# Output projections of a hybrid attention block in a score tile, and the differential tiles' results transposed within the next tile

## The chip, the cores and the metric

One core of a Trainium2 chip runs the whole kernel. The metric is the device time of one execution in microseconds (us). The kernel before takes 808.14 us, the median of three runs (807.63 to 808.69).

## The reference

One decoder block over x of 1024 tokens by 1024 features, in float32. A normalised stream is projected, the columns are split into two groups of heads, each group's result is gated, and one output projection adds both to x:

```python
h = rms_norm(x, norm_g[layer])
proj = h @ w_in[layer]
dq, dk, dv, dz, nq, nkv, nz, ng = jnp.split(proj, IN_SPLITS, axis=-1)
...
o_diff = diff_attention(dq, dk, dv, lam, diff_slopes)
o_diff = rms_norm(o_diff, diff_subln_g[layer]) * (1.0 - lam_init)
o_diff = o_diff.transpose(0, 2, 1, 3).reshape(B, T, DIFF_WIDTH) * jax.nn.silu(dz)
...
o_nsa = g[0] * o_cmp + g[1] * o_slc + g[2] * o_win
o_nsa = o_nsa.transpose(0, 3, 1, 2, 4).reshape(B, T, NSA_WIDTH) * jax.nn.silu(nz)
x = x + jnp.concatenate([o_diff, o_nsa], axis=-1) @ w_out[layer]
```

Differential attention has four heads of two causal softmax maps each; its result is softmax(first) - lambda softmax(second), times a value of width 128, and every head's result is divided by its root mean square. The native sparse attention (NSA) has eight query heads and three branches: compressed blocks, selected blocks, and a window of 512.

## The kernel before

The core works in three phases. Until about 440 us it projects the stream. Then a loop over eight tiles of 128 query tokens does NSA. At last a loop over the same eight tiles, from tile 7 down to tile 0 (`order`), does differential attention; tile `qt` sees `qt + 1` blocks of 128 keys, so tile 7 is the widest.

Both attention loops use `softmax_pair`: for two maps, TensorE computes scores into score tiles (L465, tiles S), as two matmuls for each piece since a query is kept as a high and a low part, QH and QL. VectorE adds the position bias and takes the extremum (L469, `nm`; a small second instruction reads the accumulated value), and ACT takes the exponential (L471). In the differential loop the two maps of a head are combined: VectorE works out the factor (L774, L775), POOL (L778, L779) and VectorE (L781) combine one half each. Then TensorE transposes the probabilities (L786), ACT or VectorE evicts them (L522, L520), and TensorE multiplies them by the values into a value tile O (L790). In NSA the transposes are L649 and the value matmuls L654.

When O of a differential tile is done, a norm chain runs: ACT squares it (L795), VectorE sums (L797) and mixes (L799, L800), POOL takes a power (L802), VectorE scales the factor and multiplies (L803, L804), and POOL multiplies by the gate (L806). `finish` then transposes the result on TensorE (L155), splits it in a high part `ch` (ACT, L748) and a low part `cl` (VectorE, L749), and calls `out_proj`: for each of two halves of 512 columns 12 matmuls (L502 to L504), an add to `xt` on VectorE (L505), which came by DMA, and a store (L506). `finish` of a tile is called after the heads of the next tile. In the NSA loop `out_proj` of a tile is called after the next tile's value matmuls.

PSUM has eight banks: two score tiles of two banks each (`S_tile`), two tiles for transposes of one bank each (`T_tile`), and two value tiles of one bank each (`A_tile`). O is a value tile, and so is each half of a projection, and the four transposes of the NSA gates (L696).

`load_w_out` loads the output weights in four row blocks and splits each of eight units in a high part on ACT (L488) and the rest on POOL or VectorE (L490). The order of the instructions on each engine is set by a scheduler, which places them by the program's order, its own estimates and the buffers; so the order written in the code is a priority and not the order on the engines.

Of the kernel before, what the change touches and what calls it, by code (L numbers as in the profile page):

```python
# [10 lines left out]
AF = mybir.ActivationFunctionType  # L11
# [16 lines left out]
def block_kernel(ctx: ExitStack, tc: tile.TileContext, x, norm_g, w_in, dq_g, dk_g, lq1, lk1, lq2, lk2,  # L28
                 sub_g, nq_g, nk_g, cmp_pos, cmp_w1, cmp_b1, cmp_w2, w_out, out):
    nc = tc.nc  # L30
    x = x[0]
    out = out[0]
# [13 lines left out]
    def S_tile():  # L46
        return psS.tile([128, 1024], F32, tag="S", name="S")
# [4 lines left out]
    def A_tile():  # L52
        return psA.tile([128, 512], F32, tag="A", name="A")

# [42 lines left out]
    xa_d = dram.tile([NT, 128, 1024], F32, name="xa_d")  # L97
# [69 lines left out]
    with ExitStack() as p1:  # L167
        big = p1.enter_context(tc.tile_pool(name="p1big", bufs=1))
# [4 lines left out]
        st = ctxS.enter_context(tc.tile_pool(name="p1s", bufs=2))  # L173
# [32 lines left out]
        def mm_tokens(hi, lo, tt, n):  # L206
            A = acc_tile()
            t0 = 128 * tt
            for k in range(8):
                a, b = xh[:, k, t0:t0 + 128], xl[:, k, t0:t0 + 128]  # L210
                nc.tensor.matmul(A[:, :n], a, hi[:, k, :n], start=(k == 0), stop=False)  # L211
                nc.tensor.matmul(A[:, :n], a, lo[:, k, :n], start=False, stop=False)  # L212
                nc.tensor.matmul(A[:, :n], b, hi[:, k, :n], start=False, stop=(k == 7))  # L213
            return A

# [32 lines left out]
        with ExitStack() as pc:  # L248
# [5 lines left out]
            for tt in range(NT):  # L254
# [7 lines left out]
                A = mm_tokens(*w_c0, tt, 384)  # L262
# [42 lines left out]
        for tt in range(NT):  # L305
            A = mm_tokens(*w_c1, tt, 408)
# [81 lines left out]
        for th in range(2):  # L388
            for g in range(4):
                A = acc_tile()  # L390
                for k in range(8):
                    a, b = hi[:, k, 128 * g:128 * g + 128], lo[:, k, 128 * g:128 * g + 128]
# [17 lines left out]
        for tt in range(NT):  # L410
            A = mm_tokens(*w_dz, tt, 512)
# [40 lines left out]
        def softmax_pair(QH, QL, heads, slopes, Ks, w0, biases, n, ssums, Ps):  # L452

            if n <= 512:
                S = S_tile()
                S = S[:, :512], S[:, 512:]
            else:
                S = S_tile(), S_tile()

            o = 128 if n == 640 else 0  # L460
            parts = [(c, min(c // 512 * 512 + 512, o + max(n, 256))) for c in range(o, o + n, 512 - o)][:2]
            for a in range(2):
                for c0, c1 in parts:
                    for Q in (QH, QL):
                        nc.tensor.matmul(S[a][:, c0:c1], Q[:, heads[a]], Ks[a][:, w0 + c0 - o:w0 + c1 - o],  # L465
                                         start=Q is QH, stop=Q is QL)
            for a in range(2):
                nm = small.tile([128, 1], F32, tag="nm", name="nm", bufs=8)
                nc.vector.tensor_tensor_reduce(out=Ps[a][:, :n], in0=S[a][:, o:o + n], in1=biases[a], scale=-slopes[a],  # L469
                                               scalar=3e38, op0=ALU.add, op1=ALU.min, accum_out=nm)  # L470
                nc.scalar.activation(Ps[a][:, :n], Ps[a][:, :n], AF.Exp, scale=-1.0, bias=nm, accum_out=ssums[a])  # L471

        def load_w_out(pool, raws, k0, tag, bufs):

            woh = pool.tile([128, 4, 1024], F32R, name="woh")
            wol = pool.tile([128, 4, 1024], F32R, name="wol")
            for k in range(4):

                rows = raws.tile([128, 1024], F32, tag=tag, name="wrow", bufs=bufs)
                if k0:  # L480
                    for j in range(2):
                        r0 = 512 + 256 * j + 64 * k
                        nc.sync.dma_start(rows[64 * j:64 * j + 64], w_out[r0:r0 + 64])
                else:
                    pools["wo_last"] = nc.sync.dma_start(rows, w_out[128 * k:128 * k + 128])
                for nh in range(2):
                    c = slice(512 * nh, 512 * nh + 512)
                    nc.scalar.activation(woh[:, k, c], rows[:, c], AF.Copy)  # L488
                    eng = nc.vector if k0 else nc.gpsimd
                    eng.tensor_tensor(wol[:, k, c], rows[:, c], woh[:, k, c].bitcast(F32), op=ALU.subtract)  # L490
            return woh, wol

        def out_proj(pool, ch, cl, wo, src, dst, xbufs):

            woh, wol = wo
            xt = pool.tile([128, 1024], F32, tag="xt", name="xt", bufs=xbufs)
            nc.sync.dma_start(xt, src)
            for nh in range(2):
                A = A_tile()
                c = slice(512 * nh, 512 * nh + 512)  # L500
                for k in range(4):
                    nc.tensor.matmul(A, ch[:, k], woh[:, k, c], start=(k == 0), stop=False)  # L502
                    nc.tensor.matmul(A, ch[:, k], wol[:, k, c], start=False, stop=False)  # L503
                    nc.tensor.matmul(A, cl[:, k], woh[:, k, c], start=False, stop=(k == 3))  # L504
                nc.vector.tensor_tensor(xt[:, c], A, xt[:, c], op=ALU.add)  # L505
                nc.sync.dma_start(dst[:, c], xt[:, c])  # L506
# [156 lines left out]
        pools, early = {}, {}  # L663
        for tt in range(NT):
# [5 lines left out]
            A = mm_tokens(*w_dv, tt, 512)  # L670
# [10 lines left out]
    with ExitStack() as p2:  # L681
        pools["w"] = p2.enter_context(tc.tile_pool(name="p2w", bufs=1))
        pools["rings"] = 2
        keep = p2.enter_context(tc.tile_pool(name="p2k", bufs=1))
        pools["ring"] = p2.enter_context(tc.tile_pool(name="p2r", bufs=1))
        st = p2.enter_context(tc.tile_pool(name="p2s", bufs=2))
        vsw = pools["ring"].tile([128, 2, NT, 128], F32, name="vsw")
        nc.sync.dma_start(vsw, v_d)
        wo_n = load_w_out(keep, pools["w"], 4, "bs", 2)
        pending = None  # L690
        for qt in range(NT):
            t0 = 128 * qt
            QH, QL, nzt, gate, pg, rep = nxt
            Tp = A_tile()
            for g in range(4):
                nc.tensor.transpose(Tp[:, 128 * g:128 * g + 128], pg[:, g].rearrange("p k c -> p (k c)"), ident)  # L696
            pT = pT_tile("pcT")
            nc.scalar.activation(pT, Tp, AF.Copy)
            O = A_tile()
            nc.tensor.matmul(O, vcbd, pT, start=True, stop=False)  # L700
            if qt + 1 < NT:
                nxt = cmp_branch(qt + 1)


            for br in (1, 0):
                for gp in range(2):
                    Ps = early.pop((qt, br, gp), None) or nsa_softmax(qt, br, gp, QH, QL, gate, rep)
                    nsa_values(qt, br, gp, Ps, O)
            if pending:
                out_proj(*pending)  # L710
            nc.vector.tensor_tensor(nzt, O.rearrange("p (g q) -> p g q", g=4), nzt, op=ALU.mult)
            ch = st.tile([128, 4, 128], F32R, tag="ch", name="ch")
            cl = st.tile([128, 4, 128], F32R, tag="cl", name="cl")
            nc.scalar.activation(ch, nzt, AF.Copy)
            nc.gpsimd.tensor_tensor(cl, nzt, ch.bitcast(F32), op=ALU.subtract)
            pending = (st, ch, cl, wo_n, x[t0:t0 + 128], xa_d[qt], 1)
        O_first = A_tile()
        out_proj(*pending)

    nctx.close()  # L720


    with ExitStack() as p3:
        kp = p3.enter_context(tc.tile_pool(name="p3k", bufs=1))
        p2p = p3.enter_context(tc.tile_pool(name="p3p", bufs=1))
        pools["rings"] = 1
        big = p3.enter_context(tc.tile_pool(name="p3big", bufs=1))
        st = p3.enter_context(tc.tile_pool(name="p3s", bufs=1))
# [4 lines left out]
            nc.sync.dma_start(dv[:, tt], dv_d[tt])  # L733
        for m in range(4):
            k_load(dkB[:, m], "dk", 4 + m)
        wo_d = load_w_out(big, p2p, 0, "P2", 7)

        def loads(qt):
            Q = q_stack(qs_d["dq"][qt])
# [4 lines left out]
        def finish(sq, qt):  # L744
            T3 = transposed(sq, 4)
            ch = st.tile([128, 4, 128], F32R, tag="ch", name="ch", bufs=2)
            cl = st.tile([128, 4, 128], F32R, tag="cl", name="cl", bufs=2)
            nc.scalar.activation(ch, T3, AF.Copy)  # L748
            nc.vector.tensor_tensor(cl, T3, ch.bitcast(F32), op=ALU.subtract)  # L749
            out_proj(st, ch, cl, wo_d, xa_d[qt], out[128 * qt:128 * qt + 128], 2)  # L750

        post = None
        order = (7, 6, 5, 4, 3, 2, 1, 0)
        nxt = loads(order[0])
        for i, qt in enumerate(order):
            t0 = 128 * qt
            n = t0 + 128
# [8 lines left out]
            for h in range(4):  # L766
# [6 lines left out]
                c = small.tile([128, 1], F32, tag="dc", name="dc")  # L773
# [8 lines left out]
                for k4 in range(0, qt + 1, 4):  # L782
# [5 lines left out]
                    for k in range(kn):  # L788
                        kt = k4 + k
                        nc.tensor.matmul(O[:, 128 * h:128 * h + 128], pT[:, 128 * k:128 * k + 128],  # L790
                                         dv[:, kt, 128 * h:128 * h + 128], start=(kt == 0), stop=(kt == qt))
            if post:
                finish(*post)
            sq = st.tile([128, 512], F32, tag="sq", name="sq", bufs=2)
            nc.scalar.activation(sq, O, AF.Square)  # L795
            ss = small.tile([128, 4], F32, tag="oss", name="oss")
# [8 lines left out]
                                    r[:, :, None].to_broadcast([128, 4, 128]), op=ALU.mult)  # L805
            nc.gpsimd.tensor_tensor(sq, sq, gz, op=ALU.mult)  # L806
            post = (sq, qt)
        finish(*post)


_INS = ['x', 'norm_g', 'w_in', 'diff_q_norm_g', 'diff_k_norm_g', 'diff_lambda_q1', 'diff_lambda_k1',
# [20 lines left out]
```

## Time and profile before

| | |
|---|---|
| median of three runs | 808.14 us |
| the profiled execution, device time | 807.29 us |
| its span | 805.6 us |
| TensorE matmuls busy | 770.8 us (96%) |
| VectorE busy | 516.6 us (64%) |
| ACT busy | 356.6 us (44%) |
| POOL busy | 329.1 us (41%) |

PE is TensorE's matmuls, PEld its weight loads, which lie beside them; DVE is VectorE, SP issues DMAs. An instruction's duration is from its start to its modelled end. Matmuls are pipelined, so that the distance between two starts is shorter than the duration.

### The profile page before, as it was taken

How to read it: one execution, taken by the hardware profiler on the slowest of the kernel's cores; microseconds unless marked ns; L12 is line 12 of the kernel's file. 1: busy time of each engine (PE TensorE's matmuls, PEld its weight loads, DVE VectorE, ACT ScalarE, POOL GpSimd, SP SyncE). 2: the span in 40 equal slices, each digit the busy share in tenths (PEclk: the TensorE clock that was granted, in tenths of full speed). 3: DMA queues.
4: the chain of work that ended last, by engine and by line, in shares of the span. 5: the costliest groups of instructions: out<-in, count | busy, mean ns of one | idle time of the engine just before them, and what ended most of it. 6: DMA issues, size and time to landing. Idle time of an engine off the chain costs nothing. (4 is left out here: it accounts for less than half of the span.)

```text
span 805.6 us, 13024 instructions
## 1 busy us (share of the span) xinstructions
PE 770.8 (96%) x4457; PEld 640.9 (80%) x4457; DVE 516.6 (64%) x1239; ACT 356.6 (44%) x803; POOL 329.1 (41%) x393
## 2 busy tenths in 40 slices
PE   5999999999999999999979999999999999999997
PEld 4899988888888888888757778777777668998885
DVE  4643864488634548941487687786866287789843
ACT  6443322241323223101487557565647276766410
POOL 5816272250625526020256443443342227755321
PEclk9999999999999999999999999999999999999999
DMA  8538675472433545177494232341321815556233
GB/s 286 170 58 244 165 228 140 107 195 100 138 102 112 153 100 136 40 184 207 139 216 123 84 106 81 106 91 56 80 65 34 248 34 183 159 141 172 74 130 111
DMA packets 89297, 106.68 MB, mean 132 GB/s; under 512 B 15120, under 2 KB 62352, under 8 KB 89104
## 3 DMA queue, kind: packets, MB, share of 16 engines
q1 hardware_dynamic: 89232, 105.86, 47.4%
q8 instruction: 35, 0.57, 0.3%
q14 instruction: 30, 0.25, 0.1%
HBM read 72.27 MB, written 33.55 MB: 131 GB/s over the span
## 5 line engine op out<-in xcount | busy, mean ns | idle before, releaser
L471 ACT ACTIVATE P<-P,nm 128x128 f32<-128x128 f32 (+7 forms) x136 | 101.4, 748 | 42.6 <-DVE nm L469 39.0
L203 POOL TENSOR_TENSOR wlo<-raw,whi 128x512 fp32r<-128x512 f32 (+2 forms) x64 | 85.7, 1363 | 53.1 <-ACT whi L202 51.3
L522 ACT ACTIVATE pT<-Tp 128x512 f32<-128x512 f32 (+3 forms) x118 | 66.3, 573 | 72.9 <-PE Tp L649 60.4
L138 POOL TENSOR_TENSOR r<-ss,neghalf 128x8 f32<-128x8 f32 (+2 forms) x41 | 51.0, 1244 | 112.6 <-DVE ss L136 107.6
L211 PE MATMUL S<-whi,xh 128*128 128x512 f32 (+2 forms) x224 | 86.5, 386 | 0.6 <-ACT xh L244 0.6
L211 PE MATMUL A<-whi,xh 128*128 128x512 f32 (+2 forms) x224 | 86.8, 388 | 0.0
L213 PE MATMUL A<-whi,xl 128*128 128x512 f32 (+2 forms) x224 | 86.4, 386 | 0.0
L212 PE MATMUL S<-wlo,xh 128*128 128x512 f32 (+2 forms) x224 | 86.3, 385 | 0.0
L213 PE MATMUL S<-whi,xl 128*128 128x512 f32 (+2 forms) x224 | 86.0, 384 | 0.0
L212 PE MATMUL A<-wlo,xh 128*128 128x512 f32 (+2 forms) x224 | 85.6, 383 | 0.0
L618 POOL TENSOR_SCALAR P<-P,ssum 128x128 f32<-128x128 f32 (+7 forms) x72 | 52.2, 743 | 76.4 <-DVE ssum L614 44.2
L469 DVE CUSTOM_DVE_ANT_0 P<-S,D 128x128 f32<-128x128 f32 (+7 forms) x96 | 60.3, 661 | 22.7 <-PE S L465 14.1
L465 PE MATMUL S<-nsaK,QH 128*128 128x384 f32 (+2 forms) x192 | 68.2, 363 | 0.7 <-DVE nm L469 0.7
L654 PE MATMUL A<-pT,vsw 128*64 128x256 f32 x528 | 65.4, 386 | 2.0 <-ACT P L471 1.2
L465 PE MATMUL S<-nsaK,QL 128*128 128x384 f32 (+2 forms) x192 | 60.4, 329 | 0.0
L618 POOL TENSOR_SCALAR Pw<-Pw,ssum 128x640 f32<-128x640 f32 (+3 forms) x56 | 39.8, 730 | 47.7 <-DVE ssum L614 39.8
L163 DVE RECIPROCAL e<-e 128x512 f32<-128x512 f32 (+1 forms) x18 | 57.1, 3175 | 0.5
L520 DVE COPY pT<-Tp 128x512 f32<-128x512 f32 (+3 forms) x62 | 38.5, 620 | 28.3 <-PE Tp L649 28.2
L202 ACT ACTIVATE whi<-raw 128x512 fp32r<-128x512 f32 (+2 forms) x64 | 36.5, 606 | 44.1 <-DMA raw<-in_w_in_dram 38.1
L654 PEld LDWEIGHTS A<-pT,vsw 128*64 128x64 f32 x528 | 34.6, 136 | 25.3 <-ACT pT L522 2.7
L502 PE MATMUL A<-woh,ch 128*128 128x512 f32 x128 | 51.7, 404 | 1.9 <-ACT ch L748 1.5
L504 PE MATMUL A<-woh,cl 128*128 128x512 f32 x128 | 50.3, 395 | 0.1
(189 smaller groups left out, 1772.4 us busy)
## 6 DMA issues: line engine op xcount, KB each, us to landing
raw<-in_w_in_dram SPq DMA_DIRECT2D x48, 256.0 KB, 3.1
xt<-in_x_dram SPq DMA_DIRECT2D x16, 512.0 KB, 3.8
w<-in_cmp_w_dram SPq DMA_DIRECT2D x16, 256.0 KB, 3.8
QH<-nqs_d SPq DMA_DIRECT2D x16, 256.0 KB, 5.3
QL<-nqs_d SPq DMA_DIRECT2D x16, 256.0 KB, 6.6
xa_d<-xt SPq DMA_DIRECT2D x16, 256.0 KB, 2.0
QH<-dqs_d SPq DMA_DIRECT2D x16, 256.0 KB, 5.3
QL<-dqs_d SPq DMA_DIRECT2D x16, 256.0 KB, 7.1
```

The source lines that it names most:

```text
L163: nc.vector.reciprocal(e, e)
L203: nc.gpsimd.tensor_tensor(l_, r_, h_.bitcast(F32), op=ALU.subtract)
L211: nc.tensor.matmul(A[:, :n], a, hi[:, k, :n], start=(k == 0), stop=False)
L212: nc.tensor.matmul(A[:, :n], a, lo[:, k, :n], start=False, stop=False)
L213: nc.tensor.matmul(A[:, :n], b, hi[:, k, :n], start=False, stop=(k == 7))
L465: nc.tensor.matmul(S[a][:, c0:c1], Q[:, heads[a]], Ks[a][:, w0 + c0 - o:w0 + c1 - o], start=Q is QH, stop=Q is QL)
L469: nc.vector.tensor_tensor_reduce(out=Ps[a][:, :n], in0=S[a][:, o:o + n], in1=biases[a], scale=-slopes[a], scalar=3e38, op0=ALU.add, op1=AL ...
L471: nc.scalar.activation(Ps[a][:, :n], Ps[a][:, :n], AF.Exp, scale=-1.0, bias=nm, accum_out=ssums[a])
L502: nc.tensor.matmul(A, ch[:, k], woh[:, k, c], start=(k == 0), stop=False)
L522: nc.scalar.activation(pT[:, :n], Tp[:, :n], AF.Copy)
L618: nc.gpsimd.tensor_scalar(P[:, :n], P[:, :n], ssum[:, g2, j:j + 1], 1.0, op0=ALU.mult, op1=ALU.mult)
L654: nc.tensor.matmul(O[64 * j:64 * j + 64, 256 * gp:256 * gp + 256], vsw[:, br, k0 + kt, 64 * j:64 * j + 64], pT[:, 256 * j:256 * j + 256], ...
```

## The change

`out_proj` takes one score tile and uses its two halves, where it took two value tiles. `finish` no longer calls it: it is called after the second head of the next tile, returns its arguments, and the projection is called at the end of that tile, so a tile's projection is asked for at the end of the next tile but its transposes in the middle of it; the last projections come after the loop. `load_w_out` becomes a generator that yields before each unit. The NSA weights are still split at once, the differential weights one unit per head from tile 6 on, each copy on ACT placed behind the exponential issued last. In the changed file the lines are L508 to L510 for the projection's matmuls, L511 for its add, L655 and L660 for NSA's transposes and values, L797 and L801 for the differential ones.

```diff
-                nc.scalar.activation(Ps[a][:, :n], Ps[a][:, :n], AF.Exp, scale=-1.0, bias=nm, accum_out=ssums[a])
+                exped[0] = nc.scalar.activation(Ps[a][:, :n], Ps[a][:, :n], AF.Exp, scale=-1.0, bias=nm, accum_out=ssums[a])
...
                 for nh in range(2):
+                    yield woh, wol
                     c = slice(512 * nh, 512 * nh + 512)
-                    nc.scalar.activation(woh[:, k, c], rows[:, c], AF.Copy)
+                    with tc.issue_after(exped[0].ins) if not k0 else ExitStack():
+                        nc.scalar.activation(woh[:, k, c], rows[:, c], AF.Copy)
...
+            S = S_tile()
             for nh in range(2):
-                A = A_tile()
                 c = slice(512 * nh, 512 * nh + 512)
+                A = S[:, c]
...
-        wo_n = load_w_out(keep, pools["w"], 4, "bs", 2)
+        splits = load_w_out(keep, pools["w"], 4, "bs", 2)
+        wo_n = next(splits)
+        for _ in splits:
+            pass
...
-        wo_d = load_w_out(big, p2p, 0, "P2", 7)
+        splits = load_w_out(big, p2p, 0, "P2", 7)
+        wo_d = next(splits)
...
-            out_proj(st, ch, cl, wo_d, xa_d[qt], out[128 * qt:128 * qt + 128], 2)
-
-        post = None
+            return st, ch, cl, wo_d, xa_d[qt], out[128 * qt:128 * qt + 128], 2
+
+
+        post, pending = None, []
...
-            if post:
-                finish(*post)
+                if i:
+                    next(splits, None)
+                if h == 1 and post:
+                    pending.append(finish(*post))
+            if i > 1:
+                out_proj(*pending.pop(0))
...
-        finish(*post)
+        pending.append(finish(*post))
+        for p in pending:
+            out_proj(*p)
```

The order on TensorE differs from about 440 us on. First the junction of NSA and the differential loop, on TensorE, in the kernel before. S is a score tile, dkA the keys of the first two differential heads, P and pT probabilities, vsw NSA's values.

```order
L649 MATMUL Tp<-ident,P 128x128 x16
L654 MATMUL A<-pT,vsw 64x256 x8
L649 MATMUL Tp<-ident,P 128x128 x4
L465 MATMUL S<-dkA,QH 128x512
L465 MATMUL S<-dkA,QL 128x512
...
L649 MATMUL Tp<-ident,P 128x128 x4
```

The same place in the changed kernel:

```order
L655 MATMUL Tp<-ident,P 128x128 x12
L660 MATMUL A<-pT,vsw 64x256 x8
L508 MATMUL S<-woh,ch 128x512
L509 MATMUL S<-wol,ch 128x512
L465 MATMUL S<-dkA,QH 128x512
L465 MATMUL S<-dkA,QL 128x512
...
L510 MATMUL S<-woh,cl 128x512
```

Before, scores of tile 7 stand among the last transposes of NSA; now the first of them stands behind NSA's last value matmuls and the start of its last projection.

The second place is the end of the program on TensorE, from the last value matmuls of tile 0 on. Before, where `sq` is the normalised result of a tile and dv the differential values:

```order
L504 MATMUL A<-woh,cl 128x512
L790 MATMUL A<-dv,pT 128x128 x4
L155 MATMUL Tp<-ident,sq 128x128 x4
L502 MATMUL A<-woh,ch 128x512
...
L504 MATMUL A<-woh,cl 128x512
L155 MATMUL Tp<-ident,sq 128x128 x4
L502 MATMUL A<-woh,ch 128x512
```

And after, from the last transposes of tile 1 on:

```order
L801 MATMUL A<-dv,pT 128x128
L155 MATMUL Tp<-ident,sq 128x128 x4
L797 MATMUL Tp<-ident,P_8223 128x128
L508 MATMUL S<-woh,ch 128x512
...
L801 MATMUL A<-dv,pT 128x128
L508 MATMUL S<-woh,ch 128x512
...
L510 MATMUL S<-woh,cl 128x512
L155 MATMUL Tp<-ident,sq 128x128 x4
L508 MATMUL S<-woh,ch 128x512
```

Before, all 24 matmuls of tile 1's projection lie between tile 0's last value matmul and its transposes (the first "..." of before holds 22 of them); now 12 do, those of the second half, and the first half stands among tile 0's last transposes and values.

## Rows read from the trace of the kernel before

**Rows 1.** Waits of TensorE, 645 us to the end: total, times, longest

```profile
PE S L465 <- DMA QL<-dqs_d: 2.5, 2, 1.4
PE S L465 <- DVE pT L520: 1.5, 1, 1.5
PE A L502 <- ACT ch L748: 1.5, 2, 0.8
PE S L465 <- DVE nm L469: 1.4, 1, 1.4
```

**Rows 2.** Windows: length, busy time of each engine, PEclk, DMA share, GB/s

```profile
686.00:688.00 2.00, 1.64 (x7) 1.53 (x8) 0.78 (x1) 1.01 (x3) 2.00 (x3) 0.70 1.04 413
688.00:690.00 2.00, 2.00 (x12) 2.00 (x11) 1.93 (x7) 1.78 (x4) 2.00 (x3) 0.50 1.09 256
...
720.00:740.00 20.00, 18.57 (x118) 16.52 (x117) 19.34 (x64) 13.21 (x37) 10.82 (x16) 1.00 0.71 175
```

**Rows 3.** Timeline of TensorE: start, us, engine, line, operation

```profile
666.43 0.39 PE L503 MATMUL A<-wol,ch 128*128 128x512 f32 x1
666.66 0.60 PE L786 MATMUL Tp<-ident,P 128*128 128x128 f32 x4
...
769.74 0.83 PE L790 MATMUL A<-dv,pT 128*128 128x128 f32 x6
```

**Rows 4.** Timeline of tile 2's norm chain

```profile
770.67 0.60 ACT L795 ACTIVATE sq<-A 128x512 f32<-128x512 f32 x1
...
772.26 1.01 POOL L802 TENSOR_TENSOR orr<-oss,neghalf 128x4 f32<-128x4 f32 x1 [6.19 <-DVE oss L800]
...
773.58 0.69 DVE L804 TENSOR_TENSOR sq<-A,orr 128x512 f32<-128x512 f32 x1
...
774.40 1.30 POOL L806 TENSOR_TENSOR sq<-sq,gz 128x512 f32<-128x512 f32 x1 [1.13 <-issue]
```

**Rows 5.** Timeline: chain's first and last instruction, tiles 5, 4, 1, 0

```profile
727.94 0.58 ACT L795 ACTIVATE sq<-A 128x512 f32<-128x512 f32 x1
...
738.54 1.27 POOL L806 TENSOR_TENSOR sq<-sq,gz 128x512 f32<-128x512 f32 x1
...
747.51 0.58 ACT L795 ACTIVATE sq<-A 128x512 f32<-128x512 f32 x1
...
753.60 1.30 POOL L806 TENSOR_TENSOR sq<-sq,gz 128x512 f32<-128x512 f32 x1 [1.48 <-DVE sq L804]
...
779.89 0.60 ACT L795 ACTIVATE sq<-A 128x512 f32<-128x512 f32 x1
...
783.72 1.30 POOL L806 TENSOR_TENSOR sq<-sq,gz 128x512 f32<-128x512 f32 x1 [1.06 <-issue]
...
787.72 0.60 ACT L795 ACTIVATE sq<-A 128x512 f32<-128x512 f32 x1 [3.89 <-PE A L790]
...
791.85 1.29 POOL L806 TENSOR_TENSOR sq<-sq,gz 128x512 f32<-128x512 f32 x1 [1.06 <-issue]
```

**Rows 6.** Timeline of VectorE: an extremum and its accumulator's read

```profile
658.56 1.22 DVE L469 CUSTOM_DVE_ANT_0 P<-S,D 128x1024 f32<-128x1024 f32 x1
659.70 0.08 DVE L469 DVE_READ_ACCUMULATOR2_ANT nm<- 128x1 f32 x1
```

**Rows 7.** VectorE by line and form, 640 us to the end: busy, mean ns

```profile
L469 DVE CUSTOM_DVE_ANT_0 P<-S,D 128x1024 f32<-128x1024 f32 x8 | 9.6, 1217 | 2.0 <-POOL P L779 2.0
L775 DVE TENSOR_SCALAR dc<-dc,dsum,neglam 128x1 f32<-128x1 f32 x32 | 8.6, 269 | 0.6
L469 DVE CUSTOM_DVE_ANT_0 P<-S,D 128x896 f32<-128x896 f32 x8 | 8.5, 1082 | 3.9 <-PE S L465 3.9
...
L781 DVE SCALAR_TENSOR_TENSOR P<-P,dc 128x512 f32<-128x512 f32 x6 | 5.8, 965 | 0.1
...
L774 DVE RECIPROCAL dc<-dsum 128x1 f32<-128x1 f32 x32 | 5.0, 155 | 2.0 <-ACT P L471 2.0
```

**Rows 8.** Waits of TensorE, 440 to 646 us

```profile
PE A L696 <- DVE xt L505: 1.3, 2, 1.1
```

More of the change, by code (lines that the diff above doesn't have):

```diff
@@ L470, in softmax_pair @@
                                                scalar=3e38, op0=ALU.add, op1=ALU.min, accum_out=nm)
-                nc.scalar.activation(Ps[a][:, :n], Ps[a][:, :n], AF.Exp, scale=-1.0, bias=nm, accum_out=ssums[a])
+                exped[0] = nc.scalar.activation(Ps[a][:, :n], Ps[a][:, :n], AF.Exp, scale=-1.0, bias=nm, accum_out=ssums[a])
+        exped = [None]
         def load_w_out(pool, raws, k0, tag, bufs):
@@ L486, in load_w_out @@
                 for nh in range(2):
+                    yield woh, wol
                     c = slice(512 * nh, 512 * nh + 512)
-                    nc.scalar.activation(woh[:, k, c], rows[:, c], AF.Copy)
+                    with tc.issue_after(exped[0].ins) if not k0 else ExitStack():
+                        nc.scalar.activation(woh[:, k, c], rows[:, c], AF.Copy)
                     eng = nc.vector if k0 else nc.gpsimd
                     eng.tensor_tensor(wol[:, k, c], rows[:, c], woh[:, k, c].bitcast(F32), op=ALU.subtract)
-            return woh, wol
         def out_proj(pool, ch, cl, wo, src, dst, xbufs):
```

## Prediction

> **What bounds the kernel now.** I read the waits of TensorE first, since it is by far the busiest engine: from 645 us to the end, the stretch that the change rewrites, it waits for little [rows 1]: 2.5 us for two loads of QL, 1.5 for an eviction on VectorE, 1.5 for ch behind the transposes of a finished tile, 1.4 for a score tile's extremum. In the windows from 686 to 690 us the granted clock is 0.70 and 0.50 [rows 2], the 1.2 GHz level for part of the first and all of the second, after the waits of 1.5 and 1.1 us at 684 and 686: that costs 0.3 x 2 + 0.5 x 2 = 1.6 us. So TensorE's own order, and what its next instruction waits for, sets the end. Therefore I need its pitch: a 512-wide matmul starts 0.23 us before the next [rows 3], the four transposes last 0.60 of which the last takes 0.27 in the pipe, so 0.11 each, and six value matmuls 0.83, so (0.83 - 0.28)/5 = 0.11 each, two for each block of the order. A 384-wide score matmul is estimated at 0.23 x 384/512 = 0.17, a 256-wide one at 0.12.
>
> Last comes the norm chain, the work on ACT, VectorE and POOL between a tile's last value matmul and the operand of its final transposes. In tile 2 it runs nearly undisturbed: the square starts at 770.67, the power on POOL at 772.26, the multiply at 773.58, the gate multiply at 774.40 and ends at 775.70 [rows 4], 5.03 us. In other tiles other work stands between its steps: 11.87 us in tile 5, 7.39 in tile 4, 5.13 in tile 1, 5.42 in tile 0 [rows 5], each from the square's start to the gate multiply's end. Before the change none of this is felt: TensorE has, by its order and these pitches, 5.9 to 18.8 us of other work between a tile's last value matmul and its transposes, because a whole projection (24 x 0.23 = 5.5 us) or a score stage lies there.
>
> **What the change does to the order.** The kernel issues the same instructions. The projection takes one score tile (two banks) instead of two value tiles, the transposes are asked for in the middle of the next tile rather than at its end, and the projection two tiles on. The order that results shows that the second half of this hardly happens: each projection still follows its own transposes, with one transpose group or less in between. What does change is that the transposes come sooner after the tile's last value matmul, with at most half a projection ahead of them.
>
> **A, the junction.** Before, the scores of tile 7 stand among the last NSA transposes; after, they start only behind the last NSA projection, which holds a score tile. What ends before: the wait of 1.4 for an extremum, 1.5 for the eviction, 1.1 for QL and 1.6 of clock [rows 1, 2], 5.6 in all (the second QL wait is in D). What comes: between the last NSA value matmul and its projection only the gate multiply (0.69, as the multiply in rows 4) and ch (0.60 as the square there) are left, and nothing is ahead of them on TensorE: 1.4 with hand-overs. Then from tile 7's first score to its final transposes TensorE has 62 score matmuls of 512, 16 of 384 and 14 of 256 columns, 22 of projections, 46 transposes and 46 value blocks: 14.3 + 2.8 + 1.7 + 5.1 + 5.1 + 10.1 = 39.1 us. VectorE has until tile 7's chain is through 8 extrema over 1024, 8 over 896 and 4 over 768 columns, 8 combinations of two maps, 7 operations over 512 columns, 9 pairs of small ones and 4 single small ones. Starts lie 0.08 closer than durations, as 658.56 and 659.70 show for an extremum of 1.22 [rows 6, 7]. That makes 8 x 1.14 + 8 x 1.00 + 4 x 0.87 + 8 x 0.89 + 7 x 0.61 + 9 x 0.42 + 1.3 = 37.1. It begins 0.9 later than TensorE (four matmuls), and waits, I assume, 3 us in all for probabilities of the first head; the gate multiply (1.30) then follows. 37.1 + 0.9 + 3 + 1.3 = 42.3 against 39.1: TensorE waits 3.2. A is 1.4 + 3.2 - 5.6 = -1.0. Lower end: VectorE never waits and the chain is in time, -4.2; upper end: it waits twice as long, +2.0.
>
> **B, the chains of tiles 6 to 0.** Work of TensorE between a tile's last value matmul and its transposes, after, from the order: 7.2, 5.4, 4.1, 5.4, 4.8, 3.0 and 2.75 us (tile 4: eight transposes, eight scores of 384, eight value blocks; tile 0: half a projection alone, 12 x 0.23). Against that the chain takes 5.03 at best. For the wide tiles 6 and 5 I take tile 4's 7.39, since VectorE is as loaded there; tile 5's own 11.87 stands behind a score stage that waited for QL. Stalls: 0.2 and 2.0. For tile 4 I take 6.2, the middle of 5.03 and 7.39, since the stall of tile 5 lets VectorE catch up: 2.1. Tiles 3 and 2 at 5.03: 0 and 0.2. Tile 1 at its 5.13: 2.1. Tile 0 at its 5.42: 2.7. Sum +9.3. Lower end, 5.03 everywhere: 0.9 + 0.2 + 2.0 + 2.3 = 5.4. Upper end, tile 5 at 11.87 and tile 4 at 7.39: 0.2 + 6.5 + 3.3 + 0.2 + 2.1 + 2.7 = 15.0. Behind a stalled transpose group stands everything else on TensorE, scores included, so nothing covers it, and the evictions and extrema that would have run then are late by as much.
>
> **C, behind the transposes.** The first projection matmul needs ch, 0.75 us after the last transpose (1.5 for 2 [rows 1]). The order leaves 1.1, 1.0, 0.4, 0.4, 0.3, 0.2, 0.1 and 0 us of other work there, so 0.35 x 2 + 0.45 + 0.55 + 0.65 + 0.75 = 3.1 is uncovered, against 1.5 before: +1.6. It is bounded by 0 (cl and ch wait no longer than before) and 3.1.
>
> **D, what goes.** The second QL wait, 1.4 [rows 1]: after, that load stands on SP's queue behind two weight rows and a gate and is asked for earlier than its tile. In the NSA loop the gate transposes wait 1.3 for a value tile that a projection's add still reads [rows 8]; with the projection in a score tile this ends. Sum -2.7. Upper end -1.4, when scores wait instead for the tile that the projection holds: only one other score tile is left then.
>
> **At nothing:** the split of the output weights, spread one unit per head. Its copies on ACT (0.6 each, as the square of the same size in rows 4) lie beside idle time, and its subtractions on POOL are in the same stretch as before; if ACT fell behind, the exponentials of tile 6 would be late and the stall in tile 7 longer, which A's upper end holds. DMAs are the same in number; on SP the weight rows come before tile 5's loads in both.
>
> **Sum.** -1.0 + 9.3 + 1.6 - 2.7 = +7.2 on the profiled execution's 807.29: 814.5. The median of the runs shown is 808.14, 0.85 above it, so I expect 815.3. Lower ends together: -4.2 + 5.4 + 0 - 2.7 = -1.5, 806.6. Upper ends: 2.0 + 15.0 + 1.6 - 1.4 = 17.2, 825.3.
>
> **Rivals.** *The chains are in time* (faster). If VectorE and POOL, no longer loaded by a whole projection at a tile's end, run each chain within the work that TensorE has, B and C vanish and tile 7's 3.2 with them; what stays is 1.4 - 5.6 - 2.7 = -6.9 at most, and with the stalls of tiles 1 and 0, which have only 3.0 and 2.75 us of work, about -2.1: 801.2 to 806.0, so 804. It decides in tile 4: the chain must be under 4.1 us there. Against it: the shortest chain of the trace is 5.03 [rows 4], with VectorE and POOL waiting for nothing else. For it: the waits of 1.3 and 2.5 us [rows 1, 8] go in any case.
>
> *The clock falls at the stalls.* Rows 2 show that waits of 1.5 and 1.1 us close together were followed by 4 us at or near 1.2 GHz, and cost 1.6. Three of B's stalls are that long; at 1.6 each that adds 4.8: 820.1. Against it: the second QL wait, 1.4 us long, lies in 720 to 740 us, where the clock stayed at 1.00 [rows 2]. The Trainium skill ("TensorE: Matmul & The Clock Gate", section "A second HAM failure mode: psum-queue depth-cycling") says that short idle gaps of TensorE between groups of matmuls can make the clock swing between its two levels, and that throughput is lost although single matmuls keep their time. The trace bears it out once, at 686 to 690 us.
>
> *Half of it.* Stalls at their lower ends, with C at half, B 5.4, A -1.0, D -2.7: +2.5, 810.6; with A lower still, about no change.
>
> *The deferral does nothing* is in the forecast already: the order shows it for the projections. That the score tile holds up scores is D's upper end.
>
> **How the numbers follow.** The forecast has 0.58, the clock 0.13, half of it 0.14, the chains in time 0.15. A change of under 0.2% (1.6 us) can't be told from none. The chains in time give faster, 0.15; half of it splits, 0.10 within 1.6 us and 0.04 slower; all else is slower: 0.04 + 0.58 + 0.13 = 0.75. The range leaves out the faster rival and a little above: 806.0 to 823.0; the upper end holds the clock's 820.1 and most of B's upper end.
>
> **What would show it.** Right: waits of TensorE for POOL's gate multiply ahead of the final transposes, about 2 us each in tiles 5, 4, 1 and 0, and ch waits of 3 us in eight places; no QL wait; no wait of the gate transposes in the NSA loop. If the transposes wait for nothing in tiles 1 and 0, B is wrong. If tile 7's VectorE waits for scores often, A is wrong; if NSA scores wait over 1.5 us for extrema, D is.

## The result, and the profile after

The changed kernel takes 829.16 us (median of four runs, 828.05 to 832.88) against 807.88 us of the kernel before: a ratio of 1.0275, 95% interval 1.0237 to 1.0313. The direction was forecast; the size was not: 815.3 was expected and 823 was the end of the range. The profiled execution has a span of 826.3 us against 805.6, so 20.7 us have to be found.

The waits of TensorE in the changed kernel, from 640 us to the end (total, times, longest), are those that answer to [rows 1]:

```profile
PE Tp L155 <- POOL sq L821: 11.1, 6, 2.6
PE S L508 <- ACT ch L758: 4.3, 8, 1.2
PE S L465 <- DVE nm L469: 2.3, 5, 0.7
PE S L508 <- ACT ch L723: 1.5, 1, 1.5
PE S L508 <- DVE xt L511: 1.3, 2, 0.8
PE A L660 <- DVE pT L526: 0.9, 1, 0.9
PE Tp L655 <- ACT pT L528: 0.6, 2, 0.3
```

L155 are the final transposes, L821 the gate multiply that ends the norm chain, L758 the copy ch, L511 the projection's add. With four small rows the view adds up to 23.1 us; before, from 640 us on too, it is 8.3 us (the 6.9 of [rows 1] and four small rows). So 14.8 us more are waits, and 11.1 of them stand at one instruction. The two QL waits and the eviction's 1.5 us of [rows 1] are gone, as forecast.

This is the last of the six stalls, tile 0, in the timeline of the changed kernel (start, duration, and in brackets the idle time ahead with what ended it):

```profile
809.10 0.60 ACT L810 ACTIVATE sq<-A 128x512 f32<-128x512 f32 x1 [5.18 <-PE A L801]
...
810.70 1.01 POOL L817 TENSOR_TENSOR orr<-oss,neghalf 128x4 f32<-128x4 f32 x1 [8.29 <-DVE oss L815]
...
812.01 0.69 DVE L819 TENSOR_TENSOR sq<-A,orr 128x512 f32<-128x512 f32 x1
...
812.84 1.26 POOL L821 TENSOR_TENSOR sq<-sq,gz 128x512 f32<-128x512 f32 x1 [1.13 <-issue]
...
814.15 0.66 PE L155 MATMUL Tp<-ident,sq 128*128 128x128 f32 x4 [1.60 <-POOL sq L821]
...
814.85 0.60 ACT L758 ACTIVATE ch<-Tp 128x512 fp32r<-128x512 f32 x1 [5.15 <-PE Tp L155]
...
815.50 0.50 PE L508 MATMUL S<-woh,ch 128*128 128x512 f32 x1 [0.69 <-ACT ch L758]
```

The chain runs 5.00 us, from 809.10 to 814.10, as in the undisturbed tile of [rows 4]; the transposes start 0.05 later. It is the same chain as before, now with too little work of TensorE beside it.

Part of the loss stands ahead of 440 us. The order on TensorE differs from about 410 us on, earlier than the section on the change says. Before, eight score matmuls of 384 columns stand ahead of a value matmul of NSA's compressed branch (L700, in the changed file L709), which waits for ACT; after, they stand behind it and behind the start of NSA's first projection, which holds a score tile. The last of the eight and the wait before, then the wait and the first of them after:

```profile
412.33 0.34 PE L465 MATMUL S<-nsaK,QL 128*128 128x384 f32 x1
415.30 1.12 PE L700 MATMUL A<-pcT,vcbd 128*128 128x512 f32 x2 [2.62 <-ACT pcT L698]
```

```profile
414.61 1.66 PE L709 MATMUL A<-pcT,vcbd 128*128 128x512 f32 x2 [3.98 <-ACT pcT L707]
...
419.71 0.34 PE L465 MATMUL S<-nsaK,QH 128*128 128x384 f32 x1
```

The wait is 1.4 us longer. It goes with the score tile: in the nine traces of this document whose NSA projections take one it is 3.5 to 5.4 us, in the seven with value tiles 2.1 to 3.0.

The granted clock falls at other places than in [rows 2]. Windows of the changed kernel (PEclk is the third value from the end):

```profile
404.00:406.00 2.00, 1.78 (x8) 0.75 (x8) 2.00 (x12) 2.00 (x7) 0.86 (x3) 0.71 1.02 229
406.00:408.00 2.00, 2.00 (x10) 1.78 (x12) 2.00 (x4) 2.00 (x8) 0.70 (x1) 0.50 1.03 240
...
414.00:416.00 2.00, 1.39 (x2) 0.64 (x3) 1.73 (x5) 2.00 (x9) 0.04 (x1) 0.77 1.04 236
416.00:418.00 2.00, 2.00 (x11) 1.70 (x11) 0.00 (x0) 2.00 (x7) 1.80 (x3) 0.50 0.80 188
...
790.00:792.00 2.00, 1.56 (x5) 1.37 (x6) 1.07 (x3) 0.66 (x2) 0.00 (x0) 0.63 0.94 259
792.00:794.00 2.00, 2.00 (x9) 1.81 (x8) 0.42 (x1) 0.28 (x1) 0.00 (x0) 0.51 0.38 142
...
804.00:806.00 2.00, 2.00 (x7) 1.70 (x7) 0.77 (x2) 0.00 (x0) 0.00 (x0) 0.55 0.92 343
806.00:808.00 2.00, 2.00 (x7) 1.56 (x6) 0.00 (x0) 0.00 (x0) 0.00 (x0) 0.60 0.02 7
```

The last four windows follow the final transposes of tiles 2 and 1, which waited 1.25 and 2.55 us; they cost (0.37 + 0.49 + 0.45 + 0.40) x 2 = 3.4 us. The transposes that waited 2.52, 2.12, 1.10 and 1.60 us were followed by no fall. The first four windows, ahead of 440 us, cost 3.0. The kernel before has, beside the 1.6 us of [rows 2], one more such stretch, of 1.6:

```profile
34.00:36.00 2.00, 1.92 (x10) 1.83 (x11) 0.91 (x3) 0.55 (x1) 2.00 (x3) 0.71 0.65 143
36.00:38.00 2.00, 2.00 (x9) 2.00 (x8) 0.85 (x2) 1.20 (x3) 2.00 (x3) 0.50 0.64 190
```

So the clock costs 6.5 us after and 3.2 before: 1.8 us more behind 640 us (3.4 against 1.6) and 1.5 more ahead of 440. The second part may be chance. Between 397 and 406 us both traces have nearly the same waits of TensorE (1.36, 1.06 and 0.37 us after; 1.21, 1.06 and 0.36 before), and only in the changed kernel did the clock fall; at 34 us both waited again (1.06 and 1.21), and it fell only before.

Over the whole span TensorE stands idle for 15.4 us more (50.2 against 34.8) and is busy for 5.3 us more (776.1 against 770.8), which together are the 20.7. Of the busy time the clock makes some 3.3 us. For the other 2 us no row stands alone; a part is that the first matmul after a wait is followed only 0.33 to 0.34 us later (809.57 and 815.50 are such restarts) where the pitch is 0.23.

### The profile page after: what moved, and what is told of

It is laid out like the page before. It is cut to its first block, busy times and chain, and to the rows that moved or that the text cites. A ratio compares the mean times of both kernels' runs of the same rounds, so it can differ in the third digit from the quotient of the medians.

```text
span 826.3 us, 13024 instructions
## 1 busy us (share of the span) xinstructions
PE 776.1 (94%) x4457; PEld 642.8 (78%) x4457; DVE 517.9 (63%) x1239; ACT 358.4 (43%) x803; POOL 331.3 (40%) x393
## 5 line engine op out<-in xcount | busy, mean ns | idle before, releaser
L624 POOL TENSOR_SCALAR P<-P,ssum 128x128 f32<-128x128 f32 (+7 forms) x72 | 55.0, 782 | 54.5 <-DVE ssum L620 37.5
L660 PE MATMUL A<-pT,vsw 128*64 128x256 f32 x528 | 66.7, 390 | 3.2 <-DVE pT L526 1.5
L508 PE MATMUL S<-woh,ch 128*128 128x512 f32 x128 | 53.6, 419 | 7.1 <-ACT ch L758 4.3
L660 PEld LDWEIGHTS A<-pT,vsw 128*64 128x64 f32 x528 | 34.7, 138 | 25.2 <-issue 3.0
L510 PE MATMUL S<-woh,cl 128*128 128x512 f32 x128 | 52.1, 407 | 0.0
```

Source lines behind the costliest of these rows:

```text
L624: nc.gpsimd.tensor_scalar(P[:, :n], P[:, :n], ssum[:, g2, j:j + 1], 1.0, op0=ALU.mult, op1=ALU.mult)
L660: nc.tensor.matmul(O[64 * j:64 * j + 64, 256 * gp:256 * gp + 256], vsw[:, br, k0 + kt, 64 * j:64 * j + 64], pT[:, 256 * j:256 * j + 256], ...
```

## The experiments

Three theories were compared. T: the final transposes come too soon after a tile's last value matmul, so that TensorE waits for the norm chain. S: the projection keeps one of the two score tiles from the scores. U: the split of the weights by units. Ratios are to the kernel before on the same chip.

**The parts of the change, one at a time.** Score tile alone (`e1_stile`):

```diff
+            S = S_tile()
             for nh in range(2):
-                A = A_tile()
                 c = slice(512 * nh, 512 * nh + 512)
+                A = S[:, c]
```

> The projection in a score tile alone; transposes and projection stay at the next tile's end, weights as before. Before takes 807.9 us, the whole change 829.2. Theory T (the final transposes come too soon after a tile's last value matmul): the order leaves 5.5 to 18.7 us of work ahead of every group of final transposes, more than the chains of 5 to 8 us nearly everywhere, so the waits for the gate multiply vanish; what is left is the junction and the score tile that the projection holds, 808 to 813. Rival S (the score tile that a projection holds back from the scores is the cost): most of the loss is here, 820 or more, as waits of score matmuls for an extremum or for the projection's add.

Measured: 841.25 us, ratio 1.0407 (1.0350 to 1.0465). The waits for the gate multiply are gone, as T said, but the time is far above T's interval. It is in S's (820 or more), though the waits that S named are hardly there: score matmuls wait 1.1 us from 640 us on. By line, TensorE from 640 us on (busy, mean ns, then the idle time ahead and what ended it):

```profile
L791 PE MATMUL A<-dv,pT 128*128 128x128 f32 x288 | 43.0, 292 | 7.5 <-DVE pT L521 4.2 <-ACT pT L523 3.4
...
L787 PE MATMUL Tp<-ident,P 128*128 128x128 f32 x144 | 25.9, 285 | 7.3 <-POOL P L780 5.4 <-DVE P L782 1.0 <-DVE pT L521 0.4
```

It is the transposes and values of the probabilities that wait, 14.8 us in all, of the 33.7 by which the spans differ. In the order of this kernel the first scores of a tile stand among and behind the matmuls of a projection that was asked for ahead of them and takes one of the two score tiles; that projection needs the norm chain, the transposes and ch, so the next tile's softmax starts late, and TensorE runs out of probabilities. This is read from the order and the waits; it was not tried apart. Why the whole change costs less is not shown either, since in the changed kernel too each projection follows its own transposes.

The deferral alone (`e2_defer`), with the projection in value tiles:

```diff
...
-            if post:
-                finish(*post)
+                if h == 1 and post:
+                    pending.append(finish(*post))
+            if i > 1:
+                out_proj(*pending.pop(0))
...
```

> The final transposes after the second head of the next tile and the projection two tiles on, alone: projections in value tiles, weights as before. The order leaves 8.4, 11.2, 7.1, 6.4, 4.4, 3.9, 3.0 and 2.75 us of TensorE's work ahead of the final transposes of tiles 7 to 0. Theory T: waits for the gate multiply of about 1 to 2.5 us in tiles 3 to 0, 6 to 9 in all, and some 2.5 for ch: 816 to 820, more if the clock falls. Rival S: no loss without the score tile, 808 or less.

Measured: 826.51 us, ratio 1.0251 (1.0201 to 1.0301), above T's interval, and the waits stand at another instruction than T said. The waits of TensorE from 645 us on:

```profile
PE A L502 <- DVE sq L806: 9.1, 4, 3.4
PE S L465 <- DVE nm L469: 2.3, 3, 1.4
PE Tp L155 <- POOL sq L808: 1.6, 1, 1.6
```

L806 is the chain's multiply here, which reads the value tile O. A projection in value tiles needs that bank, and waits for the chain at its first matmul; only in tile 0 do the transposes themselves wait. It is the norm chain in both kernels, at one step or the other.

The units alone (`e3_units`):

```diff
+                    yield woh, wol
...
+                if i:
+                    next(splits, None)
+                    next(splits, None)
...
```

> The split of the differential output weights by units alone, two units per head of tile 6 (the projection of tile 7 needs all eight by that tile's end), everything else as before. Theory T and rival S: nothing in it, within 3 us of before, and the order of the rest is nearly that of before. Rival U (the copies on ACT and the differences on POOL delay exponentials and norm chains): 812 or more.

Measured: 809.11 us, ratio 1.0043 (1.0018 to 1.0067), 3.3 us above the 805.77 of the kernel before on that chip: just outside what T gave, and below U's 812. The new wait in its trace is for a QL load:

```profile
PE S L465 <- DMA QL<-dqs_d: 3.6, 1, 3.6
```

It doesn't account for the 3.3 us, since the two QL waits and the eviction's of [rows 1] are gone: from 640 us on the waits add up to 8.4 us, against 8.3 before. What does differ is the mean granted clock, 0.9943 over the ten runs against 0.9970 over the nineteen of before, which makes some 2 us.

**The transposes moved back, the rest kept** (`e5_late`):

```diff
-                if h == 1 and post:
-                    pending.append(finish(*post))
             if i > 1:
                 out_proj(*pending.pop(0))
+            if post:
+                pending.append(finish(*post))
...
+        out_proj(*pending.pop(0))
         pending.append(finish(*post))
```

> The changed kernel with one thing moved: the final transposes are asked for at the next tile's end, behind the projection of the tile before, so that a whole projection lies between. Score tile and units stay. The order leaves 5.9 to 16.7 us ahead of the final transposes. Theory T: the waits for the gate multiply (11.1 us) go, those for ch fall from 4.3 to about 1.5, the clock stays at 1.00 in the last tiles: 829.2 - 11.1 - 2.8 - 3 = 812, with the junction still in it (809 to 815). Rival S: the score tile is still held, 822 or more.

Measured: 812.05 us, ratio 1.0065 (1.0043 to 1.0086), T's figure. The waits of TensorE from 640 us on hold no wait for the gate multiply any more:

```profile
PE S L508 <- ACT ch L758: 3.6, 4, 1.8
PE S L508 <- DVE xt L511: 1.6, 2, 0.8
PE S L508 <- ACT ch L723: 1.5, 1, 1.5
```

Seventeen of the 21 us hang on where the transposes are asked for. Behind 640 us the granted clock is below 0.98 in no window of 2 us of this trace. That ch falls to 1.5 was wrong (3.6).

**The chain made longer, in both.** `e9_gate_twice` and `e10_late_gate_twice` add one line to the changed kernel and to `e5_late`:

```diff
             nc.gpsimd.tensor_tensor(sq, sq, gz, op=ALU.mult)
+            nc.gpsimd.tensor_tensor(sq, sq, gz, op=ALU.mult)
```

> The changed kernel with POOL's gate multiply done twice in every tile (the gate then counts squared): each norm chain is 1.3 us longer. The order leaves 10.7, 6.5, 3.8, 3.6, 5.6, 4.8, 3.3 and 2.75 us ahead of the final transposes. Theory T: the longer chain is felt in full in seven tiles, and the waits for it go from 11.1 to about 22: 838 to 842. Rival (the chain is not on the path, something else delays both): 832 or less.

> e5_late with the gate multiply done twice in every tile, so that e9_gate_twice's edit stands where 5.9 to 17.1 us of other work lie ahead of the final transposes. Theory T: the longer chain is covered, at most 0.5 us each in the last two tiles: 811 to 814. Rival P (the added work on POOL itself costs the time, by delaying the halves of the probabilities that POOL combines): 818 or more.

Measured: 851.65 us (ratio 1.0560, 1.0531 to 1.0588) and 812.65 us (1.0079, 1.0052 to 1.0105). The same 1.3 us per tile costs 22.5 us where little work covers the chain, and 0.6 where a projection does. The waits of TensorE from 640 us on, first of `e9_gate_twice`:

```profile
PE Tp L155 <- POOL sq L822: 18.2, 7, 5.1
...
PE Tp L155 <- DVE os L814: 2.6, 1, 2.6
```

and of `e10_late_gate_twice`:

```profile
PE Tp L155 <- POOL sq L822: 0.9, 2, 0.6
```

The waits at the transposes, 20.8, are what T gave (22); the time is 10 us above it. The mean granted clock is 0.975 in `e9_gate_twice` and 0.991 in the changed kernel, over some 850 and 826 us: that is 21.2 against 7.4 us lost to the clock, idle stretches included. The 13.8 us between them and the 9.7 us of waits make the 23.5 us by which the spans differ.

**The score tile in NSA.** `e7_late_nsa_value` gives NSA's projections their value tiles back in `e5_late`; `e8_late_nsa_value_rows` has the weights by rows too; `e11_after_nsa_value` makes the first edit in the changed kernel.

```diff
-            S = S_tile()
+            S = S_tile() if xbufs == 2 else None
...
-                A = S[:, c]
+                A = S[:, c] if S is not None else A_tile()
```

> As e5_late, but NSA's projections stay in value tiles; only the differential ones use a score tile. What is left of the loss in e5_late (812.1 against 805.8) is either the junction (theory J: the scores of tile 7 stand behind NSA's last projection, which held a score tile; also the 1.6 us wait for that projection's add in the NSA loop) or lies in the last tiles (rival: ch and the projection's add, about 3 us). J: the scores of tile 7 stand among NSA's last transposes again, 806 to 809. Rival: 810 to 813.

> As e7_late_nsa_value, but the output weights are split by rows as before, so that what is left of the change is the score tile of the differential projections, two tiles on, behind late transposes. Theory U (the units cost the 3 us that e3_units showed): 3 us below e7_late_nsa_value, at or below before, 802 to 806. Rival: the same as e7_late_nsa_value within 1.5 us.

> The changed kernel with NSA's projections back in value tiles; the rest of the change stays. Theory J (the junction costs the 6.3 us by which e7_late_nsa_value lies below e5_late): 829.2 - 6.3 = 823; the order leaves 1.6 and 1.1 us less ahead of the final transposes of tiles 5 and 4 than in the changed kernel, so 823 to 826. Rival (the 6 us belong to the late transposes together with the value tiles): 828 to 831.

Measured: 805.75 us (ratio 1.0000, 0.9980 to 1.0020), 810.88 us (1.0043, 1.0023 to 1.0063) and 830.58 us (1.0289, 1.0256 to 1.0323). The first is as J said: with late transposes, 6.3 us by the medians (5.2 by the ratios, since the two ran on different chips) lay in NSA's score tile, and without it the kernel takes what before takes. The second is against U: without the units the time is 5.1 us longer (3.5 by the ratios). In its trace QH and QL come late again:

```profile
PE S L465 <- DMA QH<-dqs_d: 1.6, 1, 1.6
...
PE S L465 <- DMA QL<-dqs_d: 1.1, 1, 1.1
```

These 2.7 us, for the scores of tile 5, stand against one wait of 0.7 for QH in `e7_late_nsa_value`, and the granted clock falls behind them (0.50 and 0.66 from 690 to 694 us). So the units seem to help or hurt by where they put loads; that the work on ACT has no part in it was not tried. The third is against J: in the changed kernel the same edit brings nothing. There its order leaves less ahead of the transposes of tiles 5 and 4, and single waits for the chain grow to 4.6 us; that the two effects offset each other was not tried apart. In its trace the clock falls in four places behind 640 us, in the changed kernel's in two.

**The two halves of a score tile.** In `e7_late_nsa_value` the second half of a projection waits for the first half's add, although they lie in two banks (timeline of TensorE and VectorE in the last but one projection):

```profile
787.42 0.39 PE L510 MATMUL S<-woh,cl 128*128 128x512 f32 x1
...
787.85 0.69 DVE L511 TENSOR_TENSOR xt<-S,xt 128x512 f32<-128x512 f32 x1 [0.56 <-PE S L510]
...
788.60 0.51 PE L508 MATMUL S<-woh,ch 128*128 128x512 f32 x1 [0.78 <-DVE xt L511]
```

In the kernel before, with two value tiles, there is no such wait (a half's last matmul starts at 791.86, the next half's first at 792.08). Moving both adds behind all 24 matmuls takes it away:

```diff
-                nc.vector.tensor_tensor(xt[:, c], A, xt[:, c], op=ALU.add)
+            for nh in range(2):
+                c = slice(512 * nh, 512 * nh + 512)
+                nc.vector.tensor_tensor(xt[:, c], S[:, c], xt[:, c], op=ALU.add)
```

It was done in the changed kernel (`e12_after_adds_last`), in the score tile alone (`e14_stile_adds_last`) and in `e7_late_nsa_value` (`e15_late_nsa_value_adds_last`, where it holds for the value tiles too).

> The changed kernel with the two adds of a projection behind all 24 matmuls instead of one behind each half, so that the second half of the score tile no longer waits for the first half's add. Theory H (that wait, 1.3 us where the trace shows it, and the order it forces, is a large part of the loss): 822 to 827. Theory T: without that wait the order puts both halves ahead, and only 5.2, 4.1, 3.3, 2.8, 1.0 and 0.5 us are left ahead of the final transposes of tiles 5 to 0; with chains of 5 to 7.5 us the waits for them go from 11.1 to about 20: 835 to 841.

> e1_stile (841.3, the score tile alone) with the adds behind all 24 matmuls. Theory H (the halves of one score tile follow each other with an add between): 834 or less. Theory K (a projection that follows its own transposes holds one of two score tiles, while its ch and cl and the scores of the next heads wait; probabilities and their evictions come late): 837 to 843, with the waits for POOL's and the evictions' probabilities still there.

> e7_late_nsa_value (805.8) with the adds of the projections behind all 24 matmuls, in value tiles too. Theory H: the two waits of 0.8 us for the first half's add in the last two projections go: 803 to 804.8, a little under before. Rival (what they gave comes back elsewhere): 805 to 807.

Measured: 852.43 us (ratio 1.0548, 1.0512 to 1.0584), 849.38 us (1.0525, 1.0498 to 1.0553) and 805.93 us (0.9982, 0.9964 to 1.0000). H fell in the first two. In the first the order lets both halves go ahead, and the waits for the chain double, as T said, with the clock's 0.974 on top:

```profile
PE Tp L155 <- POOL sq L823: 23.4, 6, 5.6
```

`e14_stile_adds_last` is above K's interval too: K has the sign, not the size. In `e15_late_nsa_value_adds_last` the two waits of 0.8 us went, as H said. The median is the rival's, the ratio lies 0.0018 below that of `e7_late_nsa_value`, some 1.5 us, which would be H's, and the intervals overlap: it is not told apart from `e7_late_nsa_value`, nor clearly from before.

**Work in the place of the waits.** Transposes of the identity without use, 12 in the changed kernel (`e16_filler`) and 24 in `e9_gate_twice` (`e17_gate_twice_filler`):

```diff
...
         def finish(sq, qt):
+            if qt <= 5:
+                F = T_tile()
+                for k in range(12):
+                    with tc.issue_after(vals[0].ins):
+                        nc.tensor.transpose(F[:, 128 * (k % 4):128 * (k % 4) + 128], ident, ident)
             T3 = transposed(sq, 4)
...
```

> The changed kernel with twelve transposes of the identity, whose result nobody reads, ahead of the final transposes of tiles 5 to 0: 1.3 us of work each where TensorE waits 1.1 to 2.6 us for the norm chain. Theory C (the granted clock, whose mean is 0.991, falls because of these waits; it costs (1 - 0.991) x 826 = 7.4 us against 3.2 before): the waits for the gate multiply fall from 11.1 to 3 to 5, the mean clock rises to 0.995 or more, and the time is 824 to 828 although six times 1.3 us of work were added. Rival (the clock has nothing to do with the waits): the waits shorten, the clock stays, 829 to 830. Rival (the chain is not what TensorE waits for): 837.

> e9_gate_twice (851.7; mean clock 0.975, which costs 21 us) with 24 such transposes, 2.6 us, ahead of the final transposes of tiles 5 to 0, where it waits 1.3 to 5.1 us. Theory C: the clock rises to 0.985 or more, 838 to 846, though 15.7 us of work were added. Rival (clock and waits have nothing to do with each other): 851 or more.

Measured: 831.53 us (ratio 1.0314, 1.0293 to 1.0335) and 849.28 us (1.0519, 1.0485 to 1.0552). Neither came to the time that C gave. The waits for the gate multiply, first `e16_filler`, then `e17_gate_twice_filler`:

```profile
PE Tp L155 <- POOL sq L828: 6.8, 4, 3.3
```

```profile
PE Tp L155 <- POOL sq L829: 9.4, 6, 3.3
```

They fell by 4.3 and 11.4 us for 7.9 and 15.7 us of added work, and the mean clock rose, from 0.991 to 0.994 and from 0.975 to 0.987. So 3.6 us of added work were not covered in the first, and 4.3 in the second. The medians are 2.4 us above and 2.4 us below those of the kernels without the added work, on other chips and with overlapping intervals of the ratios, so neither difference is clear of noise. That the clock comes back where the waits go is plain in the second: 0.983 to 0.993 over its four runs, against 0.975 to 0.977. In the first the runs nearly touch (0.991 to 0.994 against 0.990 to 0.992). What it is worth by itself stays open, since the order and the waits of single tiles changed as well (tile 4's grew from 2.1 to 3.3 us in the first).

## Why the prediction was right, and where it was wrong

- **The order and what it means: right.** The rival that was named for the other side, chains that are in time, is ruled out by the waits of 1.1 to 2.6 us ahead of the transposes of tiles 5 to 0, and by `e5_late`.
- **B, the chains: right in size, and within its bounds.** Forecast 9.3 us, measured 11.1: 0, 2.5, 2.1, 1.1, 1.25, 2.55 and 1.6 in tiles 6 to 0, where 0.2, 2.0, 2.1, 0, 0.2, 2.1 and 2.7 had been forecast. The chains were 7.86, 6.10, 6.13, 5.94, 5.73 and 5.00 us in tiles 5 to 0, where 7.39, 6.2, 5.03, 5.03, 5.13 and 5.42 had been taken from the rows before. The undisturbed length was too good for tiles 3 to 1.
- **C, ch: too small, within its bounds.** 4.3 - 1.5 = 2.8 us, against 1.6 forecast.
- **A, the junction: the size was right, the place of the cost was not.** The wait for ch after NSA came as reckoned (1.5 against 1.4), and the old waits of 4.0 went. But VectorE's lateness did not show at tile 7's transposes (0 against 3.2): it shows at the scores (2.3 us in five waits for nm). Evictions and transposes wait 2.6 us, where the small rows before add up to 1.4. Without the clock A is 1.5 + 2.3 + 2.6 - 4.0 - 1.4 = +1.0, where 0.6 had been summed.
- **D, what goes: failed.** The waits of the gate transposes for a value tile went [rows 8], and the second QL wait as well. In their place came a score matmul in the NSA loop that waits 1.6 us for the projection's add, and 1.3 us of such waits at the end. D is -1.4 - 1.3 + 1.6 + 1.3 = +0.2, not -2.7, and above its upper end of -1.4: the shortage moved from one kind of tile to the other. The waits between 440 and 640 us in the changed kernel:

```profile
PE S L465 <- DVE xt L511: 1.6, 1, 1.6
```

- **The clock: the term that was furthest off.** The sum took the 1.6 us of [rows 2] as gained and put a falling clock into a rival of its own. The gain came, but so did the fall behind the stalls, 3.4 us: behind 640 us the clock is +1.8, not -1.6. It fell at two of the six stalls, not at all of them, so it belonged into the sum with a probability. The rule of the Trainium skill that stood beside that rival (page "TensorE: Matmul & The Clock Gate", section "A second HAM failure mode: psum-queue depth-cycling") is borne out in part by the windows above: after waits of 1.25 and 2.55 us the clock was at 0.51 to 0.63, after four others it did not fall.
- **Ahead of 440 us: no term.** The sum began at 440 us. The wait at L709 is 1.4 us longer there, and the clock costs 1.5 more, which may be chance.
- **At nothing: the units.** Not shown for the whole change, since `e3_units` and `e8_late_nsa_value_rows` have different signs.

The terms as measured, 1.0 + 11.1 + 2.8 + 0.2 + 1.8 = 16.9 us, stand beside the forecast's 0.6 + 9.3 + 1.6 - 2.7 - 1.6 = 7.2; with 2.9 us ahead of 440 us they make 19.8 of the 20.7. All five were forecast too low. The step that failed is the reckoning of what the change sets free: D and the clock were summed as gains of 4.3 us and measured as losses of 2.0. A, B and C lie within the bounds that were given. Of the 13.5 us that the sum lacks D and the clock make 6.3, A, B and C 3.4, and the stretch ahead of 440 us 2.9; 0.9 us is open.

## What to carry to other kernels

A tile that TensorE waits for through other engines needs as much of TensorE's own work beside it as that chain takes: count, in the order on the engine, what lies between the last matmul that feeds the chain and the first that needs it, and compare it with the chain's length in the trace, not with its undisturbed minimum. Moving a dependent step earlier in the program gains nothing where the chain sets when it can run, and everything queued behind it on the engine is late. Where stalls are forecast, give the clock's loss a term of its own in the sum, with a chance: here it came after two of six stalls, 1.7 us each.

## What was not expected of the hardware and the program

- A longer chain cost more than itself: 9.7 us more waits in `e9_gate_twice` came with a mean clock of 0.975 in place of 0.991, and the span grew by 23.5 us.
- Waits of about the same length brought a fall of the clock in one execution and none in another (at 34 us and at 397 to 406 us, above).
- The halves of one score tile, two banks, are not independent as scheduled: the second half's first matmul starts 0.06 us after the first half's add has ended (788.60 against 788.54). Two value tiles in the kernel before run on without a gap.
- The score tile alone is worse (841.25 us) than the whole change: parts that cost 35 and 21 us alone cost 21 together.
